# A distance of its own for each group's, gate head's and pair's weight parts in a two-layer hybrid trunk

## The chip, the cores and the metric

The kernel runs on one core of a Trainium2 chip. The metric is device time in microseconds (us), the median of several runs. TensorE (PE) multiplies: each matmul has a stationary operand of 128 x 128, loaded ahead of it by an instruction of its own (PEld in the profile), and a moving operand that streams through. VectorE (DVE) and ScalarE (ACT) do the elementwise work, SyncE (SP) issues most transfers.

## What is computed

The input is a residual stream x of 256 positions and 2048 channels, in fp32. Layer 0 is a Mamba-2 mixer, layer 1 a sparse latent attention; after each, x is scaled by alpha, the mixer's output is added and the sum is normalized.

```python
def ssd_mixer(x, w_in, ...):
    proj = x @ w_in
    z, xbc, dt = jnp.split(proj, [4096, 4096 + 6144], -1)
    xbc = jax.nn.silu(causal_depthwise_conv(xbc, conv_w, conv_b))
    ...
    y = ssd_chunked(xs, dt, a, bm, cm, chunk) + d_skip * xs
    yg = (y * jax.nn.silu(z)) ; yg = yg * lax.rsqrt(mean(yg * yg per group) + RMS_EPS) * norm_g
    return yg @ w_out

def dsa_mixer(x, w_in, ...):
    c_q, c_kv, k_idx, w_idx, gate = jnp.split(x @ w_in, ...)
    c_q, c_kv = rms_norm(c_q, q_norm_g), rms_norm(c_kv, kv_norm_g)
    ...
    sel = top_k(index scores, 64)
    o = attention over sel: 32 heads of 128, keys and values from c_kv, queries from c_q
    return (o * jax.nn.silu(gate)) @ w_out

x = layer_norm(ALPHA * x + mixer(x), ln_g, ln_b)
```

## The kernel before

**Weights as a stream.** All large weight matrices come as units of 128 x 1024 fp32 (half a megabyte), 404 in all. `Stream` (line 70) holds them in order. For each unit `load` fetches it into a raw tile, `convert` writes its rounded part (hi) with ACT and the remainder (lo) with DVE, up to four units (`SPLIT`) ahead of TensorE, and `run` calls the unit's own function that issues its matmuls. Activations are split into hi and lo in the same manner, and a product is made of three matmuls: hi x hi, lo x hi and hi x lo, all in the format float32r. Side work (convolutions, heads, norms) is written as generators, which `run` advances by one step after each unit, so its matmuls stand between those of two units.

**The stages, in order.** Layer 0's projection: 8 groups (g) of 20 units each. Two units make a block of 128 output channels: `stream_w` (line 301) issues 48 matmuls, the weights being the stationary operand (`hi` at L321, `lo` at L317), and 256 positions of xT the moving one. Then layer 0's output projection, 64 units, in which the activations are stationary and 512 columns of weights move (`out_proj`, L538 to L540). Then layer 1: eight units for the query latents and eight for the keys' latents (L688 to L690), 32 gate heads of two units each (again `stream_w`, now with x1T), four index units (L805 to L807), and 16 pairs of heads. A pair has a unit for keys and values (`pair_a`: keys at L868 to L870 with the weights stationary and the keys' latents ckvT moving, values at L877 to L879 the other way round) and a unit for queries (`pair_b`, L890 to L892, weights stationary, the query latents cqT moving). Heads run beside the units: logits at L928 to L931 (stationary hq, moving hk), outputs at L967 to L970 (stationary hv, moving prT). Last comes layer 1's output projection, whose final four units have tiles of their own (`st.homes`), and whose last matmuls are cut into 256 columns.

**Where operands lie.** A part's tile is 1088 columns wide, 64 more than the weights in it. The use of a unit decides at which column the weights begin (`places`, line 116): MOVING at 0, STILL (stationary) at 16, KEYS in two halves of 512 that begin at columns 32 and 576. Small tiles called gap0, gap1, gap2 and gap3 hold nothing; they shift what is allocated behind them. In the program's memory map, counted in fp32 columns modulo 64 (256 bytes), the parts' tiles, xT, x1T, yg, og and cqT begin at 0, ckvT at 16, the heads' keys hk and values hv at 48, their queries hq at 0, and the transposed probabilities prT at 32. The pool of the last four units begins behind the latents, at 16, and their weights at column 48 of it, that is 64, or 0.

Of the kernel before, what the change touches and what calls it, by code (L numbers as in the profile page):

```python
# [9 lines left out]
F32 = mybir.dt.float32  # L10
# [6 lines left out]
P = 128  # L17
# [42 lines left out]
MOVING, STILL, KEYS = range(3)  # L60


class Unit:


    def __init__(self, src, width, pe, use):
        self.src, self.width, self.pe, self.use = src, width, pe, use


class Stream:  # L70
# [7 lines left out]
        self.limit = 1 << 30  # L78
        self.homes = {}

    def add(self, src, width, pe, use):
        self.units.append(Unit(src, width, pe, use))
        return len(self.units) - 1

    def side(self, i, gen, behind=False):
# [29 lines left out]
    def places(self, i):  # L115

        u = self.units[i]
        if i in self.homes:
            pool, o = self.homes[i]
            t = [pool.tile([P, 1088], F32R, tag=k, name=f"{k}{i}") for k in ("hi", "lo")]  # L120
        else:
            o = 16 if u.use == STILL else 0
            t = [pool.tile([P, 1088], F32R, tag=k, name=f"{k}{i}")
                 for pool, k in ((self.whi, "hi"), (self.wlo, "lo"))]
        if u.use == KEYS:
            return [a.rearrange("p (a b) -> p a b", a=2)[:, :, 32:544] for a in t]
        return [a[:, o:o + u.width] for a in t]

    def finish(self, i, eng):
# [34 lines left out]
def trunk_kernel(ctx: ExitStack, tc: tile.TileContext, x, xt, w1, wdt, dtp, prm, wo1,  # L164
# [14 lines left out]
    st = Stream(nc, wraw, whi, wlo)  # L179
# [123 lines left out]
    def stream_w(half, cell, name, turn=True):  # L303


        def pe(h, l):
            if half == 0:
                cell["ps"] = acc_tile(name)[:, 0:T]
            ps, xs = cell["ps"], cell["x"][0]
            first, second = (1, 0) if half and turn else (0, 1)  # L310
            for lo in (first, second):
                for k in range(8):
                    kt = half * 8 + k
                    last = half == 1 and lo == second and k == 7
                    wt = (l if lo else h)[:, k * P:(k + 1) * P]
                    if lo:
                        nc.tensor.matmul(ps, wt, xs[:, kt, 0:T], start=False,  # L317
                                         stop=last, skip_group_check=True)
                    else:
                        for c in range(2):  # L320
                            nc.tensor.matmul(ps, wt, xs[:, kt, c * T:(c + 1) * T],  # L321
                                             start=(kt == 0 and c == 0), stop=last and c == 1,
                                             skip_group_check=True)
        return pe
# [183 lines left out]
    for g in range(NG):  # L508
        for kind, n in (("B", 1), ("C", 1), ("x", 4), ("z", 4)):
            for ci in range(n):  # L510
                cell = {"x": xcell}
                for half in range(2):
                    k = len(st.units)
                    i = st.add(w1[k], 1024, stream_w(half, cell, f"acc{k}", turn=k > 1), STILL)
                if kind == "z":
                    st.side(i, (z_steps, g, ci, cell))
                else:
                    cc = {"x": g * 4 + ci, "B": 32 + g, "C": 40 + g}[kind]
                    st.side(i, (conv_steps, g, kind, ci, cc, cell))
# [202 lines left out]
    def add_gate(h):  # L722
        cell = {"x": xcell}
        for half in range(2):
            i = st.add(wg[h * 2 + half], 1024, stream_w(half, cell, f"g{h}"), STILL)
        st.side(i, (gate_steps, h, cell))


# [69 lines left out]
    def idx_pe(q, cell):  # L798
        def pe(h, l):
            cell["ps"] = acc_tile(f"ix{q}")  # L800
            for k in range(2):
                ps = cell["ps"][:, k * T:(k + 1) * T]
                for kt in range(4):
                    o = (k * 4 + kt) * P
                    nc.tensor.matmul(ps, h[:, o:o + P], cqT[:, kt, 0:T], start=(kt == 0), stop=False)  # L805
                    nc.tensor.matmul(ps, h[:, o:o + P], cqT[:, kt, T:2 * T], start=False, stop=False)
                    nc.tensor.matmul(ps, l[:, o:o + P], cqT[:, kt, 0:T], start=False, stop=(kt == 3))  # L807
        return pe
# [40 lines left out]

    for q in range(4):  # L850
        cell = {}
        i = st.add(wix[q], 1024, idx_pe(q, cell), STILL)
        st.side(i, (idx_steps, q, cell))
    st.side(i + 5, (top_steps,), behind=True)
    for _ in range(5):
# [67 lines left out]
    def head_steps(h):  # L923
        p, k = divmod(h, 2)
        (qh, ql, q1), (kh, kl, k1) = ([a[:, k, :] for a in PR[p][nm]] for nm in "qk")
        vh, vl, v2 = (a[:, k * P:(k + 1) * P] for a in PR[p]["v"])
        pl = y_tile(f"lg{h}")
        nc.tensor.matmul(pl[:, 0:128], q1, k1, start=True, stop=True)  # L928
        nc.tensor.matmul(pl[:, 128:384], qh, kh, start=True, stop=False)
        nc.tensor.matmul(pl[:, 128:384], qh, kl, start=False, stop=False)  # L930
        nc.tensor.matmul(pl[:, 128:384], ql, kh, start=False, stop=True)  # L931
        yield
        lg = d2.tile([P, 384], F32, tag="lg", name=f"lgs{h}")
        mx = d2.tile([P, 2], F32, tag="mx", name=f"mx{h}")
        sm = d2.tile([P, 2], F32, tag="sm", name=f"sm{h}")
        rn = d2.tile([P, 2], F32, tag="rn", name=f"rn{h}")
        parts = ((0, 0, 128), (1, 128, 384))
        for j, a, b in parts:
            v.tensor_tensor_reduce(out=lg[:, a:b], in0=pl[:, a:b], in1=mb[:, a:b],
                                   scale=-ATT_SCALE, scalar=3.0e38, op0=ALU.add, op1=ALU.min,  # L940
                                   accum_out=mx[:, j:j + 1])
        yield
        for j, a, b in parts:
            nc.scalar.activation(lg[:, a:b], lg[:, a:b], AF.Exp, scale=-1.0,
                                 bias=mx[:, j:j + 1], accum_out=sm[:, j:j + 1])
        yield
        v.reciprocal(rn, sm)
        for j, a, b in parts:
            v.tensor_scalar(lg[:, a:b], lg[:, a:b], rn[:, j:j + 1], 0.5,
                            op0=ALU.mult, op1=ALU.mult)  # L950
        yield
        yield
        pt = m_tile(f"pt{h}")
        for a in (0, 128, 256):
            nc.tensor.transpose(pt[:, a:a + 128], lg[:, a:a + 128], ident)  # L955
        yield
        if h == 0:
            d2.tile([P, 48], F32, tag="gap3", name="gap3", bufs=1)
        ph, pl = (d2.tile([P, T], F32R, tag=f"prT{j}", name=f"prT{h}_{j}") for j in range(2))
        p2 = d2.tile([P, P], F32, tag="prT2", name=f"prT{h}_2")  # L960
        nc.scalar.activation(ph, pt[:, 0:T], AF.Copy)
        nc.scalar.activation(p2, pt[:, T:384], AF.Copy)
        v.tensor_sub(pl, pt[:, 0:T], ph.bitcast(F32))
        yield
        yield
        po = y_tile(f"o{h}")
        nc.tensor.matmul(po[:, 0:T], vh, ph, start=True, stop=False)  # L967
        nc.tensor.matmul(po[:, 0:T], vh, pl, start=False, stop=False)
        nc.tensor.matmul(po[:, 0:T], vl, ph, start=False, stop=False)
        nc.tensor.matmul(po[:, P:T], v2, p2, start=False, stop=True)  # L970
        yield
        og = d2.tile([P, T], F32, tag="og", name=f"og{h}")
        v.tensor_mul(og, po[:, 0:T], GT.pop(h))
        if h == 0:
            OG.append(big.tile([P, KT, 2 * T], F32R, tag="A", name="og0"))
        if h == 16:
            OG.append(big.tile([P, KT, 2 * T], F32R, tag="C", name="og1"))
        dst = OG[h // 16][:, h % 16, :]
        yield
        nc.scalar.activation(dst[:, 0:T], og, AF.Copy)  # L980
        yield
        v.tensor_sub(dst[:, T:2 * T], og, dst[:, 0:T].bitcast(F32))
        yield
# [2 lines left out]
    left = NH2 - 8  # L986
    for p in range(NH2 // 2):
        src = wab[2 * p]
        i = st.add(wab[2 * p], 1024, pair_a(p), KEYS)
        st.side(i, (evac_steps, p, ("k", "v")))  # L990
        i = st.add(wab[2 * p + 1], 1024, pair_b(p), STILL)
        st.side(i, (evac_steps, p, ("q",)))
        st.side(i + 3, (head_steps, 2 * p))
        st.side(i + 5, (head_steps, 2 * p + 1))
        n = (left * (p + 1)) // 16 - (left * p) // 16
        for _ in range(n):
            add_gate(next(gates))
# [138 lines left out]
    lat = ctx.enter_context(tc.tile_pool(name="lat", bufs=1))  # L1136
    lat.tile([P, 56], F32, tag="gap0", name="gap0")
    cqT = lat.tile([P, 4, 2 * T], F32R, tag="cqT", name="cqT")
    lat.tile([P, 16], F32, tag="gap1", name="gap1")
    ckvT = lat.tile([P, 2, 2 * T], F32R, tag="ckvT", name="ckvT")  # L1140
    A.update(ckvT=ckvT, cqT=cqT)
    mb = lat.tile([P, 384], F32, tag="mb", name="mb")
# [199 lines left out]
```

## Time and profile before

| | us |
|---|---|
| median of three runs | 1234.57 |
| lowest, highest | 1232.88, 1234.94 |
| the profiled execution | 1232.97 |
| its span, from the first to the last instruction | 1231.1 |

The profile describes the one profiled execution. Its page gives busy times of each engine, and a chain: starting from the last instruction, it goes back at each step to whatever released that instruction, or to the one before it on its engine. The chain's list names pieces with their start, their length in us and how many instructions they hold (x32). Because a piece ends where the next begins, its length over its count is the pace at which instructions followed each other. In the timeline the second column is different: it runs to the end of the last instruction, and neighbouring matmuls overlap, so there the pace is read from the starts.

### The profile page before, as it was taken

The numbers are of one execution on the slowest core, as the hardware profiler recorded it, in microseconds if no ns is written. First come the engines' busy times: TensorE is split into PE (matmuls) and PEld (weight loads), VectorE is DVE, ScalarE is ACT, GpSimd is POOL, SyncE is SP. The second block draws the span as 40 slices with busy tenths as digits, with TensorE's granted clock in tenths as the row PEclk, the third lists the DMA queues.
The fourth block names the chain that finished last, engine by engine and source line by source line (L and its number), as shares of the span: only waits on it lengthen the run. The fifth ranks groups of instructions, "written<-read, shape, count | busy, mean of one in ns | idle before, by whom it ended". The sixth has DMA issues, their size and how long they took to land.

```text
span 1231.1 us, 22869 instructions
## 1 busy us (share of the span) xinstructions
PE 1224.9 (100%) x8981; PEld 1143.1 (93%) x8981; DVE 900.1 (73%) x1644; ACT 666.9 (54%) x1163; POOL 65.4 (5%) x102
## 2 busy tenths in 40 slices
PE   9999999999999999999999999999999999999998
PEld 8999999999999999788888899999999999888886
DVE  7977778888788878756557768867777777567457
ACT  5555555655565556444336655566666666433441
POOL 0001011001100110110000000000000001000000
PEclk9999999999999999999999999999999999999999
DMA  8766566566656665566666564555554555875662
GB/s 296 229 195 195 187 200 189 177 204 203 190 181 203 200 193 181 188 226 231 192 197 201 200 205 149 180 162 160 156 155 148 161 155 187 312 228 187 201 192 97
DMA packets 65371, 236.77 MB, mean 192 GB/s; under 512 B 8024, under 2 KB 8160, under 8 KB 64880
## 3 DMA queue, kind: packets, MB, share of 16 engines
q1 hardware_dynamic: 60352, 215.29, 54.5%
q0 software_dynamic: 4912, 20.02, 5.0%
q8 instruction: 71, 1.16, 0.4%
q14 instruction: 36, 0.29, 0.1%
HBM read 231.00 MB, written 4.28 MB: 191 GB/s over the span
## 4 chain that ended last, share of the span: by engine, by line
PE 99%; DMA 1%; SPq 0%; DVE 0%; ACT 0%; DVEq 0%; issue 0%
PE acc L321 24%; PE acc L317 12%; PE g L321 10%; PE o L538 9%; PE o L540 9%; PE o L539 9%; PE g L317 5%; PE y L436 2%; PE q L891 1%; PE q L890 1%; PE q L892 1%; PE pt L955 1%; PE pxs L416 1%; PE v L878 1%; PE v L879 1%; PE v L877 1%
## 5 line engine op out<-in xcount | busy, mean ns | idle before, releaser
L131 DVE TENSOR_TENSOR lo<-raw,hi 128x1024 fp32r<-128x1024 f32 (+1 forms) x404 | 489.7, 1215 | 273.1 <-ACT hi L109 270.9
L109 ACT ACTIVATE hi<-raw 128x1024 fp32r<-128x1024 f32 (+1 forms) x403 | 421.8, 1051 | 216.5 <-PE o L540 158.6
L321 PE MATMUL acc<-xT,hi 128*128 128x256 f32 x2560 | 316.7, 280 | 0.2 <-ACT hi L106 0.2
L321 PEld LDWEIGHTS acc<-xT,hi 128*128 128x128 f32 x2560 | 303.7, 188 | 2.3 <-ACT E L391 1.2
L317 PE MATMUL acc<-xT,lo 128*128 128x256 f32 x1280 | 162.5, 279 | 0.0
L317 PEld LDWEIGHTS acc<-xT,lo 128*128 128x128 f32 x1280 | 154.1, 188 | 0.0
L321 PE MATMUL g<-x1T,hi 128*128 128x256 f32 x1024 | 127.9, 280 | 0.0
L321 PEld LDWEIGHTS g<-x1T,hi 128*128 128x128 f32 x1024 | 122.0, 188 | 0.2
L538 PE MATMUL o<-hi,yg 128*128 128x512 f32 x256 | 100.3, 392 | 0.0
L539 PE MATMUL o<-lo,yg 128*128 128x512 f32 x256 | 99.6, 389 | 0.0
L540 PE MATMUL o<-hi,yg 128*128 128x512 f32 x256 | 99.6, 389 | 0.0
L538 PE MATMUL o<-hi,og 128*128 128x512 f32 (+1 forms) x256 | 99.5, 389 | 0.0
L540 PE MATMUL o<-hi,og 128*128 128x512 f32 (+1 forms) x256 | 98.9, 386 | 0.0
L539 PE MATMUL o<-lo,og 128*128 128x512 f32 (+1 forms) x256 | 98.8, 386 | 0.0
L340 DVE SCALAR_TENSOR_TENSOR ca<-acc,par,ca 128x255 f32<-128x255 f32 x144 | 69.0, 479 | 3.4
L317 PE MATMUL g<-x1T,lo 128*128 128x256 f32 x512 | 69.4, 280 | 0.0
L317 PEld LDWEIGHTS g<-x1T,lo 128*128 128x128 f32 x512 | 63.4, 188 | 0.2
L538 PEld LDWEIGHTS o<-hi,yg 128*128 128x128 f32 x256 | 48.1, 188 | 10.1 <-issue 0.2
L540 PEld LDWEIGHTS o<-hi,yg 128*128 128x128 f32 x256 | 48.1, 188 | 10.0
L539 PEld LDWEIGHTS o<-lo,yg 128*128 128x128 f32 x256 | 48.1, 188 | 9.9
L540 PEld LDWEIGHTS o<-hi,og 128*128 128x128 f32 x256 | 48.1, 188 | 9.6
L539 PEld LDWEIGHTS o<-lo,og 128*128 128x128 f32 x256 | 48.1, 188 | 9.6
(270 smaller groups left out, 1660.5 us busy)
## 6 DMA issues: line engine op xcount, KB each, us to landing
raw<-in_w_dram SPq DMA_DIRECT2D x160, 512.0 KB, 4.1
raw<-in_wo_dram SPq DMA_DIRECT2D x128, 512.0 KB, 4.2
raw<-in_wg_dram SPq DMA_DIRECT2D x64, 512.0 KB, 3.5
raw<-in_wab_dram SPq DMA_DIRECT2D x32, 512.0 KB, 3.7
abc<-acs_d POOLq DMA_DIRECT2D x32, 256.0 KB, 4.3
raw<-in_wcq_dram SPq DMA_DIRECT2D x8, 512.0 KB, 4.4
raw<-in_wkv_dram SPq DMA_DIRECT2D x8, 336.0 KB, 3.1
scr<-in_xt_dram SPq DMA_DIRECT2D x4, 512.0 KB, 6.3
```

Source lines behind the costliest of these rows:

```text
L109: self.nc.scalar.activation(h, r, AF.Copy)
L131: eng.tensor_sub(*self.halfway.pop(i))
L317: nc.tensor.matmul(ps, wt, xs[:, kt, 0:T], start=False, stop=last, skip_group_check=True)
L321: nc.tensor.matmul(ps, wt, xs[:, kt, c * T:(c + 1) * T], start=(kt == 0 and c == 0), stop=last and c == 1, skip_group_check=True)
L340: v.scalar_tensor_tensor(acc[:, d:], ps[:, :T - d], w(k), acc[:, d:], op0=ALU.mult, op1=ALU.add)
L416: nc.tensor.transpose(pm[:, o:o + P], G[g][("x", 2 * half + c)][:, s * P:(s + 1) * P], ident)
L436: nc.tensor.matmul(py[ks, c * T + s * P:(c + 1) * T], xsT[:, s, c, ks], ms[c][k][:, ws], start=(c == 0 and s == 0), stop=(s == 1), skip_gr ...
L538: nc.tensor.matmul(ps, ah, hs, start=(kk == 2 * first), stop=False)
L539: nc.tensor.matmul(ps, ah, ls, start=False, stop=False)
L540: nc.tensor.matmul(ps, al, hs, start=False, stop=(kk == 31))
L877: nc.tensor.matmul(ps, ch, h[:, 1, o:o + T], start=(ct == 0), stop=False)
L878: nc.tensor.matmul(ps, ch, l[:, 1, o:o + T], start=False, stop=False)
```

## The change

A unit gets a field `at`, the column at which its weights begin. Group g of layer 0 has 8 times g, gate head h 8 times (h modulo 8), the queries of pair p 8 times (p modulo 8); the index units keep 16. For KEYS the first half now begins at column 0 and the second at 512 + 8 times (p modulo 5). The gap ahead of ckvT grows from 16 to 48 columns, which moves ckvT, the mask and everything of the heads behind it by 32; the gap ahead of prT shrinks from 48 to 32, so prT moves by 16. Nothing else changes: the same instructions are issued in the same order.

```diff
-    def __init__(self, src, width, pe, use):
-        self.src, self.width, self.pe, self.use = src, width, pe, use
+    def __init__(self, src, width, pe, use, at):
+        self.src, self.width, self.pe, self.use, self.at = src, width, pe, use, at
...
-    def add(self, src, width, pe, use):
-        self.units.append(Unit(src, width, pe, use))
+    def add(self, src, width, pe, use, at=0):
+        self.units.append(Unit(src, width, pe, use, at))
...
-            o = 16 if u.use == STILL else 0
+            o = u.at
             t = [pool.tile([P, 1088], F32R, tag=k, name=f"{k}{i}")
                  for pool, k in ((self.whi, "hi"), (self.wlo, "lo"))]
         if u.use == KEYS:
-            return [a.rearrange("p (a b) -> p a b", a=2)[:, :, 32:544] for a in t]
+            n = 512 + u.at
+            return [a[:, 0:2 * n].rearrange("p (a b) -> p a b", a=2)[:, :, 0:512] for a in t]
...
-                    i = st.add(w1[k], 1024, stream_w(half, cell, f"acc{k}", turn=k > 1), STILL)
+                    i = st.add(w1[k], 1024, stream_w(half, cell, f"acc{k}", turn=k > 1), STILL,
+                               8 * g)
...
-            i = st.add(wg[h * 2 + half], 1024, stream_w(half, cell, f"g{h}"), STILL)
+            i = st.add(wg[h * 2 + half], 1024, stream_w(half, cell, f"g{h}"), STILL,
+                       8 * (h % 8))
...
-        i = st.add(wix[q], 1024, idx_pe(q, cell), STILL)
+        i = st.add(wix[q], 1024, idx_pe(q, cell), STILL, 16)
...
-            d2.tile([P, 48], F32, tag="gap3", name="gap3", bufs=1)
+            d2.tile([P, 32], F32, tag="gap3", name="gap3", bufs=1)
...
-        i = st.add(wab[2 * p], 1024, pair_a(p), KEYS)
+        i = st.add(wab[2 * p], 1024, pair_a(p), KEYS, 8 * (p % 5))
...
-        i = st.add(wab[2 * p + 1], 1024, pair_b(p), STILL)
+        i = st.add(wab[2 * p + 1], 1024, pair_b(p), STILL, 8 * (p % 8))
...
-    lat.tile([P, 16], F32, tag="gap1", name="gap1")
+    lat.tile([P, 48], F32, tag="gap1", name="gap1")
```

## The prediction

> **What bounds the kernel now.** I began with the page's shares of the engines, its slices and the head of the chain that ended last, then asked for the waits of TensorE.
>
> ```profile
> span 1231.1 us, 22869 instructions
> ...
> PE 1224.9 (100%) x8981; PEld 1143.1 (93%) x8981; DVE 900.1 (73%) x1644; ACT 666.9 (54%) x1163; POOL 65.4 (5%) x102
> ...
> PEclk9999999999999999999999999999999999999999
> ...
> PE 99%; DMA 1%; SPq 0%; DVE 0%; ACT 0%; DVEq 0%; issue 0%
> ```
>
> ```profile
> PE zeros L624 <- DVE scr L619: 1.3, 1, 1.3
> PE acc L321 <- ACT hi L106: 0.2, 1, 0.2
> ```
>
> TensorE's stream is the whole span: 99% of the chain, a full granted clock in each slice, and 1.5 us in which it waited for another engine, all before its first weight matmuls. So nothing that hides beside TensorE can move the time, and whatever moves it must change how closely its matmuls follow each other. The busy figure cannot show that, since neighbouring matmuls overlap in the records. The chain can: there a run of matmuls is listed with the time it really added.
>
> ```profile
> by line: PE acc L321 24.1%; PE acc L317 12.0%; PE g L321 9.6%; PE o L538 9.4%; PE o L540 9.4%; PE o L539 9.4%; PE g L317 4.8%; PE y L436 1.9%; PE q L891 1.2%; PE q L890 1.2%; PE q L892 1.2%; PE pt L955 0.9%; PE pxs L416 0.7%; PE v L878 0.6%
> ...
> 20.79 3.63 PE acc L321 x32
> 26.23 3.63 PE acc L321 x32
> 31.67 3.63 PE acc L321 x32
> 43.81 3.63 PE acc L321 x32
> 55.14 3.63 PE acc L321 x32
> 60.58 3.63 PE acc L321 x32
> ...
> 102.08 3.63 PE acc L321 x32
> 115.14 3.77 PE acc L321 x32
> 120.80 3.77 PE acc L321 x32
> ...
> 145.72 3.63 PE acc L321 x32
> ...
> 715.69 3.77 PE g L321 x32
> ...
> 757.10 3.63 PE g L321 x32
> 762.54 3.63 PE g L321 x32
> ...
> 1032.80 3.77 PE g L321 x32
> ```
>
> The reader is to see two paces of the same instruction: 3.63 us for 32, which is 113.4 ns each, and 3.77 us, which is 117.8 ns. Same line, same shape, same full clock, same place of the weights (column 16 of their tiles). What separates them is what ran before:
>
> ```profile
> 107.36 1.98 PE L321 MATMUL acc<-xT,hi 128*128 128x256 f32 x16
> 109.26 1.52 PE L436 MATMUL y<-M,xsT 128*64 128x256 f32 x16
> 110.72 0.66 PE L416 MATMUL pxs<-ident,xs 128*128 128x128 f32 x4
> 111.13 2.13 PE L321 MATMUL acc<-xT,hi 128*128 128x256 f32 x16
> 113.09 2.05 PE L317 MATMUL acc<-xT,lo 128*128 128x256 f32 x16
> ```
>
> A few side matmuls (L436, L416) cut in, and the stream, at 3.63 in the run of 102.08, goes on at 3.77 in those of 115.14 and 120.80. The slower pace then lasts until another interruption ends it. How often? The shares by line say: acc L321 24.1% of 1231.1 us over 2560 matmuls is 115.9 ns; acc L317 12.0% over 1280, g L321 9.6% over 1024 and g L317 4.8% over 512 are each 115.4 ns; q's 1.2% over 128 is also 115.4. I use 115.5 as the present mean: about half the stream at each pace, 2.2 ns above the better one.
>
> **A place in the trace with another distance.** Let the distance be the column of the stationary operand less that of the moving one, modulo 64 fp32 (256 bytes), in the program's memory map. (Modulo 64 is a choice: eight steps of 8 make 64, and no trace here shows the period.) Every tile of 1088 is a multiple of 64, and xT, x1T, cqT, yg and og begin at 0 modulo 64. So STILL weights at column 16 stand at distance 16. KEYS weights (column 32) against ckvT (16), values (16 against 576, that is 0), heads' logits (hq 0, hk 48) and outputs (hv 48, prT 32) are also at 16. MOVING weights are at distance 0, and these have 512 columns, with one exception: the 48 matmuls of 256 columns in the last projection's end.
>
> ```profile
> 1214.12 0.39 PE L539 MATMUL o<-lo,og 128*128 128x512 f32 x1
> 1214.34 0.39 PE L540 MATMUL o<-hi,og 128*128 128x512 f32 x1
> 1214.57 0.28 PE L538 MATMUL o<-hi,og 128*128 128x256 f32 x1
> 1214.68 0.28 PE L539 MATMUL o<-lo,og 128*128 128x256 f32 x1
> 1214.80 0.28 PE L540 MATMUL o<-hi,og 128*128 128x256 f32 x1
> 1214.92 0.28 PE L538 MATMUL o<-hi,og 128*128 128x256 f32 x1
> ...
> 1220.20 0.28 PE L540 MATMUL part<-hi,og 128*128 128x256 f32 x1
> ```
>
> From 1214.92 to 1220.20 are 44 steps: 120.0 ns each, nothing cutting in. That is a third pace, slower than both others, with the same shape at distance 0. The 512-column ones before it, at the same distance, start 0.22 to 0.23 us apart, two times 113 ns. I read it so: a matmul of 256 columns and the loading of the next 128 stationary columns last equally long, so a hold-up of the load shows; beside 512 columns it is hidden.
>
> **The change part by part.** No instruction, transfer or wait is added or removed; only columns move. Per distance of the eight there is one group of 20 units of 24 matmuls (480), four gates (192) and two pairs' queries (48).
>
> 1. *Distance 0.* Group 0 goes there from 16. Of its 480 matmuls the first 40 come before 17 us; the chain's x32 runs of 20.79 to 60.58 show the rest at 113.4. At 120.0 that is 440 x 6.6 = 2.9 us, and the 40 at 2.2 to 4.5 each are 0.1. Gates 0, 8, 16 and 24: 192 x (120.0 - 115.4) = 0.9. Queries of pairs 0 and 8: 48 x 4.6 = 0.2. Sum **+4.1 us**.
> 2. *Distance 16.* Group 2, gates 2, 10, 18 and 26, queries of pairs 2 and 10, and all four index units stay: 0. The keys stay too: their first half goes to column 0, and ckvT, moved from 16 to 48, keeps 0 - 48 = 16 modulo 64. The heads' logits keep 16, as hq and hk move together.
> 3. *Distances 8, 24, 32, 40, 48, 56.* Six groups (2880), 24 gates (1152), 12 pairs' queries (288), the values of 13 pairs (48 less 8 times p modulo 5; 12 matmuls each, 156) and the heads' outputs (hv 16, prT 48, so 32; 96): 4572 matmuls. The trace shows no long run at any of these. Nearest rows: at best all at 113.4, 4572 x -2.2 = -10.1 us; at worst all at 120.0, 4572 x 4.5 = +20.6 us. I take **0**, the row of distance 16: load and stream start together and the stream runs twice as fast, so from any distance but 0 it passes the load's place somewhere in the middle; only at 0 do the two stand on each other where every matmul begins. Moving the meeting from one middle place to another has no evident price.
> 4. *The end of the last projection.* Its last four units lie in a pool opened behind the latents, and that begins 32 columns later now while the column 48 within stays. So the 48 matmuls quoted go from 0 to 32: 48 x (115.5 - 120.0) = **-0.2 us**, between -0.3 and 0.
> 5. *Splitting.* ACT and DVE write the parts at other columns.
>
> ```profile
> L131 DVE TENSOR_TENSOR lo<-raw,hi 128x1024 fp32r<-128x1024 f32 (+1 forms) x404 | 489.7, 1215 | 273.1 <-ACT hi L109 270.9
> L109 ACT ACTIVATE hi<-raw 128x1024 fp32r<-128x1024 f32 (+1 forms) x403 | 421.8, 1051 | 216.5 <-PE o L540 158.6
> ```
>
> I cost that at nothing: DVE is idle 1231.1 - 900.1 = 331 us, so each of 404 subtractions could take 0.8 us longer on top of 1215 ns before DVE's sum filled the span. The cover is the four split units ahead; gone, each excess would fall on TensorE whole.
>
> The sum is +4.1 + 0 + 0 - 0.2 = +3.9 us. The profiled execution took 1232.97 us, 1231.1 of them span, which gives 1236.9; the median of the runs, 1234.57, lies 1.6 above it, and on that the forecast is **1238.5 us**.
>
> **The rivals.**
>
> *Addresses don't matter* (the change doesn't do what it says). The third pace would then come from something else in the last projection: stationary activations that alternate, say. For it: two paces exist at one distance, so history matters without any address. Against it: 120.0 holds for 44 steps, and neither 113.4 nor 117.8 appears after the third. Change 0, 1234.6 us, and what interruptions leave is the same. The Trainium skill, "TensorE: Matmul & The Clock Gate", section "Step-by-step: what each phase is for", says that TensorE reads the moving operand and the weights over two ports independent of each other; by that rule the distance costs nothing and this case holds. The 120.0 ns at distance 0 speak against it, though no run here has moved only the distance.
>
> *Distance 0 has a width.* If the load trails the stream by a little, 8 and 56 collide at the beginning or end of each matmul as 0 does. Groups 1 and 7: 960 x 4.5 = 4.3; eight gates: 384 x 4.6 = 1.8; four pairs: 96 x 4.6 = 0.4. With +3.9 that is +10.4, 1245.0 us. If only 16 is good, +3.9 + 20.6 = +24.5, 1259.1 us.
>
> *Faster: the slower pace belongs to 16.* If it arises because 16 is still close to 0, then from 24 to 56 the stream returns to 113.4 after each interruption: groups 3 to 7 (2400), 20 gates (960), ten pairs (240), values and outputs (252) are 3852 x 2.2 = 8.5 us off, and 3.9 - 8.5 = -4.6, 1230.0 us. It decides from the point where 3.9 us / 2.2 ns = 1770 matmuls, 46% of these, give up the slower pace. For it: group 0's runs and the gates' of 757.10 and 762.54 are all at 3.63, so the good pace lasts where it begins. Against it: that was at 16 as well, so what chooses is the interruption.
>
> **How the numbers follow.** My forecast (only distance 0 costs): 0.44. Its own range is 1236.5 to 1240.5, as ten points more or less of the slower pace among 4572 matmuls are 4572 x 0.1 x 4.4 ns = 2.0 us. No effect: 0.15. A width around 0: 0.17. Only 16 good: 0.06. Faster: 0.18. What this measurement can tell from no change is 0.2%, 2.5 us: 1232.1 to 1237.0. Slower takes 0.36 of the forecast's 0.44, 0.17 and 0.06: 0.59. Faster takes 0.14 of the 0.18 and 0.02 of no effect: 0.16. The same is what is left: 0.08 + 0.13 + 0.04 = 0.25. The range from 1229.5 to 1248.0 leaves out the 0.06, the lower half of the faster case (0.09) and 0.03 of the width's upper end, 0.18 in all.
>
> **What would show each step right or wrong.** In the chain of the changed kernel the x32 runs of group 0 (20 to 66 us) should read 3.84 us, those of group 2 3.63 and 3.77 as now; the 48 at the end should start 113 to 118 ns apart. Groups 1, 3, 4, 5, 6 and 7 each stand for a distance, in the order of time: 3.84 in groups 1 and 7 alone is the width, 3.63 throughout groups 3 to 7 the faster case. Group 0 still at 3.63 would end the reading of the third pace, and with it the forecast. Waits of TensorE for DVE or ACT, beyond the 1.5 us, would say that step 5 was wrong.

## The result and the profile after

The changed kernel takes 1247.23 us in the median of four runs (1246.80 to 1247.70), against 1234.00 us for the kernel before in four runs. The ratio is 1.0107, with a 95% interval of 1.0094 to 1.0119: **slower by 13.2 us**, in the direction forecast and inside the range (1229.5 to 1248.0), but more than three times the 3.9 us of the sum.

The page of the changed kernel, its engines' busy times and the head of its chain, and below them its waits of TensorE:

```profile
span 1245.8 us, 22869 instructions
...
PE 1238.5 (99%) x8981; PEld 1156.6 (93%) x8981; DVE 900.8 (72%) x1644; ACT 667.2 (54%) x1163; POOL 65.1 (5%) x102
...
PE 99%; DMA 1%; SPq 0%; DVE 0%; ACT 0%; DVEq 0%; issue 0%
```

```profile
PE zeros L626 <- DVE scr L621: 1.3, 1, 1.3
PE p_dt L615 <- DMA scr<-in_xt_dram: 0.8, 1, 0.8
PE p_dt L615 <- DMA scr<-in_wdt_dram: 0.4, 1, 0.4
PE acc L322 <- ACT hi L106: 0.2, 1, 0.2
```

Same instructions, same share of TensorE in the chain, and no new wait but 1.2 us for the first transfers at the very start. So the time is in the pace of the matmuls. The chain's list (start, us, what) has a run of 32 from every group of layer 0, that is, from every distance:

```profile
27.62 3.84 PE acc L322 x32
...
94.41 3.79 PE acc L322 x32
...
155.96 3.63 PE acc L322 x32
...
186.23 3.77 PE acc L322 x32
...
216.96 3.80 PE acc L322 x32
...
279.01 3.80 PE acc L322 x32
...
341.40 3.84 PE acc L322 x32
...
403.45 3.63 PE acc L322 x32
...
433.70 3.77 PE acc L322 x32
...
464.30 3.73 PE acc L322 x32
```

The starts lie in groups 0, 1, 2, 2, 3, 4, 5, 6, 6 and 7, so the distances are 0, 8, 16, 16, 24, 32, 40, 48, 48 and 56. Only group 2, whose distance did not change, and group 6, at 48, still have 3.63; both have 3.77 as well. To see what each part paid, I summed for each the times from one matmul's start to the next, in both traces:

```
part                     matmuls   before    after   difference, us
group 0 (distance 0)         480    55.15    58.11   +2.96
group 1 (8)                  480    56.15    57.30   +1.15
group 2 (16)                 480    56.15    56.16   +0.00
group 3 (24)                 480    56.15    57.45   +1.30
group 4 (32)                 480    56.16    57.68   +1.53
group 5 (40)                 480    56.16    58.29   +2.14
group 6 (48)                 480    56.16    56.20   +0.05
group 7 (56)                 480    56.16    56.66   +0.50
gates                       1536   179.90   184.06   +4.16
queries, keys, values        768    90.93    91.25   +0.31
index units                   96    11.50    11.17   -0.33
heads                        320    36.10    36.19   +0.10
first matmuls (zeros, dt)     76     9.87    10.56   +0.70
last 48 of 256 columns        48     5.75     5.75    0.00
all else                                             +0.15
sum                                                 +14.72
```

The sum is the growth of the span, 1245.8 - 1231.1. It exceeds the medians' 13.2 because the profiled execution of before was a quick one of its kernel (1232.97 against 1234.00), and that of the changed kernel the slowest of its four (1247.70 against 1247.23).

### The profile page after: what moved, and what is told of

Read it like the earlier page. It is cut to its first block, busy times and chain, and to the rows that moved or that the text cites. A ratio compares the mean times of both kernels' runs of the same rounds, so it can differ in the third digit from the quotient of the medians.

```text
span 1245.8 us, 22869 instructions
## 1 busy us (share of the span) xinstructions
PE 1238.5 (99%) x8981; PEld 1156.6 (93%) x8981; DVE 900.8 (72%) x1644; ACT 667.2 (54%) x1163; POOL 65.1 (5%) x102
## 4 chain that ended last, share of the span: by engine, by line
PE 99%; DMA 1%; SPq 0%; DVE 0%; ACT 0%; DVEq 0%; issue 0%
PE acc L322 24%; PE acc L318 12%; PE g L322 10%; PE o L540 9%; PE o L542 9%; PE o L541 9%; PE g L318 5%; PE y L437 2%; PE q L895 1%; PE q L893 1%; PE q L894 1%; PE pt L958 1%; PE pxs L417 1%; PE v L882 1%; PE v L880 1%; PE v L881 1%
## 5 line engine op out<-in xcount | busy, mean ns | idle before, releaser
L322 PE MATMUL acc<-xT,hi 128*128 128x256 f32 x2560 | 323.1, 282 | 0.2 <-ACT hi L106 0.2
L322 PEld LDWEIGHTS acc<-xT,hi 128*128 128x128 f32 x2560 | 309.8, 189 | 2.3 <-ACT E L392 1.2
L318 PE MATMUL acc<-xT,lo 128*128 128x256 f32 x1280 | 165.7, 281 | 0.0
L318 PEld LDWEIGHTS acc<-xT,lo 128*128 128x128 f32 x1280 | 157.1, 189 | 0.0
L322 PE MATMUL g<-x1T,hi 128*128 128x256 f32 x1024 | 130.7, 282 | 0.0
L322 PEld LDWEIGHTS g<-x1T,hi 128*128 128x128 f32 x1024 | 124.6, 189 | 0.2
L540 PEld LDWEIGHTS o<-hi,yg 128*128 128x128 f32 x256 | 48.1, 188 | 10.1 <-issue 0.2
L542 PEld LDWEIGHTS o<-hi,og 128*128 128x128 f32 x256 | 48.1, 188 | 9.9
L540 PEld LDWEIGHTS o<-hi,og 128*128 128x128 f32 x256 | 48.1, 188 | 9.5
```

Of the source, the lines that this page charges most:

```text
L318: nc.tensor.matmul(ps, wt, xs[:, kt, 0:T], start=False, stop=last, skip_group_check=True)
L322: nc.tensor.matmul(ps, wt, xs[:, kt, c * T:(c + 1) * T], start=(kt == 0 and c == 0), stop=last and c == 1, skip_group_check=True)
L540: nc.tensor.matmul(ps, ah, hs, start=(kk == 2 * first), stop=False)
L542: nc.tensor.matmul(ps, al, hs, start=False, stop=(kk == 31))
```

## The experiments

**Place or distance, and the other parts.** Two kernels take the changed one apart. The first moves the distances to other groups:

```diff
-                               8 * g)
+                               8 * ((g + 4) % 8))
```

> The changed kernel with group g at distance 8 times ((g + 4) modulo 8). If the distance sets a group's time: the group at 0 (now group 4) takes some 58.2 us between its matmuls' starts, that at 40 (now group 1) 58.3, those at 16 and 48 (now 6 and 2) 56.2, group 0 (now at 32) about 57.4; all in all 1247 us, within 1.5. If the group's place sets it (rival): group 0 stays at 58.1 and group 5 at 58.3, groups 2 and 6 at 56.2 with the others between, whatever their distance.

Measured: 1246.94 us, in one run. The group at distance 0 (now group 4) took 58.27 us, that at 40 (group 1) 58.10, those at 16 and 48 56.16 and 56.20, group 0 at 32 took 57.50. The mean pace of a group, interruptions aside, goes with the distance to a tenth of a ns: 119.9 at 0 in both kernels, 118.3 at 8, 115.4 at 16, 118.1 at 24, 118.7 and 118.6 at 32, 120.0 at 40, 115.6 at 48 and 116.7 at 56. The place is out. The second kernel undoes the groups alone:

```diff
-                               8 * g)
+                               16)
```

> The changed kernel with all eight groups of layer 0 back at distance 16; gates, pairs, latents and the rest as changed. If each part pays for its own matmuls by its own distance, the groups give back what they lost in the traces (2.96, 1.15, 0, 1.30, 1.53, 2.14, 0.05 and 0.50 us, 9.6 in all): 1237.6 us, within 1. If the stages are coupled (rival: the groups' loss is made up for or caused elsewhere), the gates' 4.2 us changes too, or the total is off by more than 2.

Measured: 1238.93 us, a ratio of 1.0035 (1.0020 to 1.0051) to the kernel before. In its trace groups 1 to 7 are back at 56.15 to 56.16 and the gates unchanged, so the parts are not coupled. The 1.3 us above the expectation are group 0: 56.40 us, not the 55.15 that it had in the trace of before, with the same distance. Two kernels further down, kick and kick2, have the group 0 of before as well: it took 56.39 and 55.13 us. In the two traces with the longer time, ssd16 and kick, TensorE had waited 1.8 and 1.1 us for the first transfers; in the other two it had not. So the pace with which the stream begins differs between traces of the same code, and here it went with the start. That the wait is the cause was not tested.

**Streams alone.** A kernel that computes nothing of the trunk issues streams of 48 matmuls, after three kinds of short interruption: four transposes (turn), two fp32 matmuls (two), eight half-width matmuls as in y (cols); the profile lists each of these fp32 matmuls as two.

```python
def run(name, s0, m0, n, w=256):
    ...
    for k in range(n):
        a, b = s0 + (k // 2 % 8) * P, m0 + (k % (4096 // w)) * w
        nc.tensor.matmul(ps, sta[:, a:a + P], mov[:, b:b + w], start=k == 0, stop=k == n - 1)
```

> Leaves out the whole computation: only streams of matmuls of 256 float32r columns, 48 to a stream, each after a short interruption of one of three kinds, at distances 0 to 60 in steps of 4, then 64 and 80; the same again with both operands moved by 8 and by 16 columns; a few streams of 512 columns; and streams whose distance changes on the way. If the distance modulo 64 sets the pace: 120.0 ns at 0 and at 64, 118.3 at 8, 113.3 or 117.8 at 16, 48 and 80, 117 to 119 at 24 and 32, 120.0 at 40, 116.7 at 56, the same with both operands moved, and 227 ns for 512 columns at every distance. If the column of the weights alone counts (rival): the streams with both operands moved by 8 take the paces of a distance larger by 8. If the period is 128 or more: 64 and 80 differ from 0 and 16.

The chain's list of this kernel; a name's letter stands for the distance over 4 (a 0, e 16, m 48, q 64, u 80), "bothb" means both operands moved by 8 columns, "wide" 512 columns:

```profile
30.24 5.74 PE da L191 x48
...
109.27 5.46 PE de L191 x48
...
116.18 5.85 PE de L191 x48
...
261.54 5.66 PE dm L191 x48
...
346.57 5.74 PE dq L191 x48
...
366.30 5.46 PE du L191 x48
...
425.37 5.47 PE bothbde L191 x48
```

```profile
695.37 5.46 PE widea L191 x24
...
719.36 5.60 PE widek L191 x24
```

Distance 64 is distance 0 and 80 is 16, to 0.01 us: the period is 64 columns. Moving both operands by 8 or 16 leaves the two paces at 16 and the 120.0 at 0; the weights' own column counts for nothing. In the second half of a stream, when it is settled, the starts are apart by 120.0 ns at 0, 118.3 at 4 and 8, 117.8 to 118.4 at 12, **113.3 or 117.8 at 16**, 118.7 at 20, 117.4 or 118.7 at 24, 119.8 to 120.3 at 28, 118.6 to 120.0 at 32, 118.3 to 120.0 at 36, 119.8 to 120.2 at 40, 118.1 at 44, **117.8 at 48**, 116.7 at 52, 116.7 or 117.8 at 56, 117.4 to 119.9 at 60. In these streams the 113.3 was nowhere but at 16 (and 80, the same), and at 48 where one at 16 had run before. The streams called go... change their distance on the way, without an interruption:

```profile
739.55 2.72 PE goad L191 x24
...
742.71 2.83 PE goba L191 x24
745.54 2.83 PE gobb L191 x24
748.37 2.83 PE gobc L191 x24
751.19 2.72 PE gobd L191 x24
...
851.94 3.02 PE goca L191 x24
854.96 0.93 PE gocb L191 x8
855.89 2.73 PE gocc L191 x24
...
861.03 3.03 PE goda L191 x24
864.06 0.95 PE godb L191 x8
865.01 2.84 PE godc L191 x24
```

"goa" (16, 48, 16, 48) keeps 113.3 to its last run at 48. "gob" (48, 16, 48, 16) keeps 117.8 through two changes and loses it at the third; after eight half-width matmuls it lost it at the first. In "goc" a stream at 16 began slow (3.02 with its start), eight matmuls at 56 followed, and then 16 ran at 113.3. The two streams after it show the limits of that. In "god" a slow stream at 48 was still at 117.8 after eight matmuls at 56, in all three cases; in "goe" a slow stream at 16 was still at 117.8 after eight at 32, in the one case in which it had begun slow. So the paces at 16 and 48 are states: which one holds depends on how the stream was entered, and it can last. One expectation failed outright: 512 columns are not at 227 ns everywhere. They are at 226.6 at distance 0 and 233.5 at 8 and 40 once settled.

**All at 48.** The kernel before, with one number changed:

```diff
-            o = 16 if u.use == STILL else 0
+            o = 48 if u.use == STILL else 0
```

> The kernel before with all STILL weights at column 48 in place of 16. If 48 is as good as 16, as the changed kernel's group 6 says (paces of 113.3 and 117.8, 56.20 us against 56.15 for group 2): 1234 us, within 2. If 16 alone is good and group 6 was so by its place: slower by 5 us and more.

Measured: 1245.45 us in two runs, ratio 1.0087 (1.0058 to 1.0117). I was wrong about it, and the chain shows how; this is group 2:

```profile
148.41 3.77 PE acc L321 x32
...
154.06 3.77 PE acc L321 x32
...
161.59 0.43 PE cb L365 x2
...
166.02 3.77 PE acc L321 x32
...
173.55 1.45 PE y L436 x16
```

In groups 1 to 7 every interruption left the stream at 117.8, also those after which 16 returns to 113.3. Group 6 of the changed kernel, at this very distance, was at 113.3 after two of its five interruptions (y, and the two fp32 matmuls of cb). What differed before them is the distance of group 5. So two distances with the same two paces are not equal: the entry counts, and in this kernel no interruption of groups 1 to 7 led 48 into its better pace.

**Alternating.** The two distances with the good pace, in turn:

```diff
-            o = 16 if u.use == STILL else 0
+            o = (16, 48)[i % 2] if u.use == STILL else 0
```

> The kernel before with STILL weights at column 16 in even units and 48 in odd ones. Both distances have the good pace of 113.3. If the pace of 117.8 is a lock of load and stream that only a constant distance keeps, changing the distance at each unit breaks it: fewer runs at 117.8, 1221 to 1230 us. If what the interruption leaves is kept whatever the distance (rival): 1234 us, within 2. If the change of distance itself throws the stream off: slower than 1236.

Measured: 1232.81 us in eight runs, ratio 0.9986 (0.9974 to 0.9997), far from the 1221 to 1230 of the first theory. The time is what the rival gave, but not by the rival's mechanism. In groups 1 to 7 slow stretches did end, at a change from 48 back to 16 and never at one from 16 to 48 (these groups gained 0.26 to 0.45 us each in the trace). But units that had been fast in the kernel before began slow, and the gates lost 1.63.

**Ending the slower pace on purpose.** If the state is what "goc" showed, eight matmuls at 56 behind an interruption that leaves 117.8 should be enough. The lo part of a unit is eight matmuls:

```diff
+KICK = {20 * g + j: 56 for g in range(1, 8) for j in ((4, 14) if g == 1 else (0, 14))}
...
-        return [a[:, o:o + u.width] for a in t]
+        return [t[0][:, o:o + u.width], t[1][:, KICK.get(i, o):KICK.get(i, o) + u.width]]
```

> The kernel before with the lo part of 14 units of layer 0 at column 56 in place of 16: those that follow an interruption after which the stream keeps 117.8 ns (units 4 and 14 of group 1, 0 and 14 of groups 2 to 7). If 117.8 is a state that a few matmuls at another distance end, as 8 at 56 did in the streams that began slow, the rest of each slow stretch runs at 113.3: 1560 slow matmuls less 14 times 24, times 4.45 ns, is 5.4 us off, 1229.3 us. If the state is tied to the interruption and comes back (rival): the 16 and 48 patterns stay, within 1 us of 1234.7. If the switch back itself costs: slower by up to 2 us.

Measured: 1233.27 us in ten runs, ratio 0.9987 (0.9978 to 0.9997): 1.5 us off, not 5.4. The chain in group 2:

```profile
142.48 2.08 PE acc L322 x16
144.56 1.88 PE acc L318 x16
146.45 3.77 PE acc L322 x32
...
173.23 1.89 PE acc L322 x16
175.12 1.86 PE acc L318 x16
176.98 3.63 PE acc L322 x32
```

Behind the unit at 173.23, which has a lo part at 56, the pace is 113.4: so it was in 14 cases of 14. But unit 4, after y, which had gone over to 113.3 in the kernel before, now stayed at 117.8 for its 144 matmuls (146.45). Mending one stretch changed how the next was entered. The trace of before already held this case: in group 1, where units 0 to 3 ran at 113.3, units 4 to 9 behind the same interruption ran at 117.8. The next kernel adds the values at distance 48, by KEYS halves without a gap, and some gate units:

```diff
+KICK.update({i: 56 for i in (240, *range(277, 340, 10))})
...
-            return [a.rearrange("p (a b) -> p a b", a=2)[:, :, 32:544] for a in t]
+            return [a[:, 32:1056].rearrange("p (a b) -> p a b", a=2) for a in t]
```

> As kick, and besides: the lo part of gate units 240 and 277, 287 to 337 at column 56, and the KEYS halves without a gap between them, so that the values' matmuls stand at distance 48 in place of 16 (the keys' stay at 16). If states are ended by another distance and the values run at 113.9 at 48, as in the changed kernel: 3 us below kick, some 1226 us. Rival: the states come back at the next interruption and the gain stays below 1 us.

Measured: 1229.85 us in five runs, ratio 0.9963 (0.9950 to 0.9976). That is the 3 us below kick that was expected, but not all of it is the edit's: in the traces group 0, the same in both kernels, took 1.26 us less than in kick, and the first matmuls 0.56. Against the kernel before, the values gained 0.72 us and the gates 0.83; units 277 to 337, whose eight come directly behind the interruption, stayed slow after them. The last one mends y's stretch too, and group 0, and leaves 277 to 337 alone:

```diff
-KICK = {20 * g + j: 56 for g in range(1, 8) for j in ((4, 14) if g == 1 else (0, 14))}
-KICK.update({i: 56 for i in (240, *range(277, 340, 10))})
+KICK = {20 * g + j: 56 for g in range(8) for j in ((1, 10) if g == 0 else (4, 14) if g == 1 else (0, 4, 14))}
+KICK.update({240: 56, 262: 56})
```

> As kick2 (values at 48), with the lo part at column 56 in units 1 and 10 of group 0, 4 and 14 of group 1, 0, 4 and 14 of groups 2 to 7, and in units 240 and 262; not in 277 to 337. In kick's trace unit 4 of groups 2 to 7 came to 117.8 for 144 matmuls once the stretch before it was mended. If that is another state to be ended: 6 times 120 times 4.45 ns = 3.2 us below kick2, 1226 to 1227 us. If each mended stretch puts a later one into the slower state (rival): 1229 to 1231 us.

Measured: **1227.68 us** in five runs, ratio 0.9943 (0.9929 to 0.9956) to the kernel before: it is faster than that and than the changed kernel. The same place of its chain as in kick:

```profile
141.67 2.08 PE acc L324 x16
143.75 1.86 PE acc L320 x16
145.61 3.63 PE acc L324 x32
```

In the whole of layer 0's projection no stretch stays at 117.8 beyond the unit that ends it. It lies about 1 us above what was expected, and as much is in the gates: 180.05 us, where kick2 had 179.07.

**Which load collides.** In a stream whose operands change columns from one matmul to the next, a matmul's own weights and the next one's stand at different distances from what it streams.

```python
for i, (ss, ms) in enumerate((((16, 32), (0, 16)), ((0, 16), (0, 16)), ((0, 48), (0, 48)),
                              ((16, 48), (0, 32)), ((48, 16), (0, 32)))):
    # matmul k: stationary at column ss[k % 2], moving at ms[k % 2]
```

> Leaves out the whole computation: streams of 48 matmuls whose two operands change columns from one matmul to the next, so that a matmul's own weights and the next one's weights, loaded beside it, stand at different distances from its moving operand; then streams of 32 matmuls of 192, 320, 384, 448 and 512 columns at distances 0, 8, 16, 40 and 48. If the load of the next weights collides with the stream beside it: own 16 with next 32 and 0 runs at 118 to 120 ns, own 0 with next 16 and 48 at 113.3 or 117.8, own 16 with next 48 and own 48 with next 16 as those two. If a matmul's own weights count (rival): own 16 at 113.3 or 117.8, own 0 at 120.0. With more columns (floors of 17/16 of the columns at 2.4 GHz: 142, 170, 198 and 227 ns at 320, 384, 448 and 512): if only the load is held up, the floor at every distance from 384 on; if the moving stream is held up too, 2 to 7 ns above it wherever the distance is not 0, as the first streams of 512 columns had it.

The chain's list ("cross" and the case's letter a to e; "w" and the columns over 64 as a letter, f 320, g 384, then the distance over 4):

```profile
54.26 5.71 PE crossa L219 x48
60.62 5.60 PE crossb L219 x48
...
141.76 4.70 PE wfa L233 x32
...
157.16 4.70 PE wfk L233 x32
...
167.42 5.58 PE wga L233 x32
...
185.46 5.66 PE wgk L233 x32
```

Settled, case a (own 16, next 32 and 0) runs at 118.8 ns and case b (own 0, next 16 and 48) at 116.8; c, d and e are at 116.6 to 116.8. Own weights alone would have given b 120.0, and it isn't there. The next ones alone would have given b 113.3 or 117.8, and that isn't there either; they give a right. The order of the two cases goes with the next weights, the sizes with neither, so this stays open. The floors that I had assumed for 320, 384 and 448 columns fell: 320 take 146.7 ns at all five distances, 384 take 173.3 at best, 448 take 200.0 at best. At 192 columns, too, the distance costs nothing: all five take 111.5 to 111.8, hardly less than 256 columns at their best. So the price of a distance is not the same at every width, and nothing here says why.

## Why the prediction was right, and where it was wrong

- **TensorE bounds, and pace decides**: right. Of the 14.7 us, all but 0.7 at the start and some 0.15 elsewhere is in matmuls of 256 columns, and TensorE gained no wait for DVE or ACT, so step 5's cover held.
- **Step 1, distance 0**: right in price and size. 4.1 us were forecast; group 0 paid 2.96 us at 119.9 ns, the four gates 0.68 at 119.8 and the queries 0.19, 3.8 in all. A part of that agreement is luck: from the 56.40 us that group 0 took in ssd16's trace it would have been 1.7 us for the group.
- **Step 2, what stays at 16**: right within 0.3 us. Group 2 paid 0.00 us, the keys 0.11. The four gates that stayed at 16 paid 0.28, since more of their matmuls ran at the slower pace, and the index units gained 0.33.
- **Step 3, the other six distances**: this failed. It was set at 0 on the argument that from any distance but 0 the meeting lies "somewhere in the middle", and that moving it "has no evident price". In groups 1 and 3 to 7 it cost 1.15 + 1.30 + 1.53 + 2.14 + 0.05 + 0.50 = 6.7 us, and in the 24 gates 3.2; with queries, values and outputs it is some 10 of the 14.7 us. All distances but 16 and 48 lack the pace of 113.3, and 40 is as bad as 0. The trace had no row for those distances; its bounds, -10.1 and +20.6, held, and so did the range. That the time lies inside the range is not owed to the sum, whose own range ended at 1240.5: it is owed to the room that was left for the rival of a width around 0.
- **Step 4, the last 48**: the step happened and brought nothing: at 32 they take 5.75 us as at 0.

```profile
1229.64 0.28 PE L540 MATMUL o<-hi,og 128*128 128x256 f32 x1
...
1233.48 0.28 PE L542 MATMUL part<-hi,og 128*128 128x256 f32 x1
```

That is 32 steps in 3.84 us in the changed kernel's timeline, 120.0 ns each.

- **The reading behind it**, that beside 512 columns a hold-up of the load is hidden, is wrong: streams of 512 columns pay up to 7 ns, and 0 is the best of the six distances tried. So what a bad distance costs is not hidden beside the longer stream; whether the load or the moving stream is held up was not shown.
- **The rivals.** "Addresses don't matter" fell with the kernel that moved the distances between the groups. The Trainium skill, "TensorE: Matmul & The Clock Gate", section "Step-by-step: what each phase is for", has two independent read ports for the two operands; these runs disagree with what I drew from it, for the distance alone moves the pace from 113.3 to 120.0 ns. "Distance 0 has a width" named too few distances, and came nearest by its sum (1245.0 us). The faster rival had it the wrong way round: away from 16 the pace of 113.3 is not regained but lost, except at 48; but its idea that the slower pace can be got rid of was sound, and kick3 did it at distance 16.
- **Two paces at one distance** were seen before the change, and rightly ascribed to interruptions. They also move the times: group 0 took 55.15 us in the profiled execution of before and 56.40 in ssd16's, at the same distance. That this, with the wait at the start, accounts for most of the 1.6 us between that execution and the median of the first runs is likely, and was not shown.

What stays open is the mechanism itself: why 16 and 48 have a good state, and how an interruption selects it.

## What to carry to other kernels

Where matmuls of 256 float32r columns follow each other, each with a load of weights of its own, the columns at which both operands begin are a tuning parameter: try their distance modulo 64, in steps of 8 or 16, and measure the whole kernel, because the state in which a stream is entered counts as much as its best pace. Read the pace from starts, or from the chain's runs, never from busy time. And when a trace holds no row for a new setting, a value that only symmetry argues for is a guess: keep the bounds.

## What the runs showed of the hardware

- The pace of such a stream depends on the operands' distance with a period of 64 fp32 columns (64 ran as 0, and 80 as 16): 113.3 to 120.3 ns, at a full granted clock.
- Many settled paces are whole multiples of 6.67 ns: 113.3 (17), 120.0 (18), 146.7 (22, 320 columns), 173.3 (26, 384 columns), 226.7 (34, 512 columns). Others are not: the slower pace at 16 and 48, 117.8, is 17 and two thirds of them, and 116.7 at 56 is 17 and a half.
- The paces at 16 and 48 are states that can last through more than a hundred matmuls (144 in kick's units 4 to 9 of a group). At 16, eight matmuls at distance 56 ended the slower one in all 22 places of layer 0 where kick3 put them, but not at once behind an interruption, as in kick2's units 277 to 337; at 48 they did not end it, and eight at 32 did not at 16. Changes from 48 to 16 ended it in some cases and not in others.
